# Forming two operand sums of a ConvFFN in PSUM and placing two steps of a third weight job ahead of them

## The chip, the cores and the metric

The kernel runs on one core of a Trainium2 chip. The metric is the device time of one execution in microseconds (us); the figure for a kernel is the median over its runs. Engines are named as the profile names them: PE is TensorE, DVE is VectorE, ACT is ScalarE, POOL is GpSimd, SP is SyncE. In this kernel SP issues nearly all of the DMAs.

## The reference

One layer of an encoder: two attention branches are merged, projected by `w_out` and added to the residual; then comes a ConvFFN whose input is a norm of that residual. The part around the change, with D_MODEL 1024, SEQ 1024, D_FF 2816 and everything in float32:

```python
x = x + gate1 * (merged @ w_out[i])
h2 = rmsnorm(x, g_ffn[i]) * (1 + scale2) + shift2
u = depthwise_conv_seq(h2 @ w_up[i], conv_w[i], conv_b[i])      # width 3, over positions
u_val, u_gate = jnp.split(u, 2, axis=-1)
x = x + gate2 * ((jax.nn.gelu(u_gate, approximate=True) * u_val) @ w_down[i])
return rmsnorm(x, g_final)
```

## The kernel before

**Number format.** A float32 operand is split into `hi` (the value rounded to the matmul's format) and `lo` (the rest). Every product is three matmuls: hi by hi, hi by lo, lo by hi (lines 77 to 79 in the projections, 916 to 918 in the later part). `split` does this for weights: ACT writes `hi` (line 55), DVE or POOL writes `lo` (line 56). `operand` (lines 862 and 863) does it for activations, and `shifted` (lines 1036 and 1037) does it while adding a shift per partition.

**Fewer products.** `h2 @ w_up` is done with seven products of half-size blocks in place of eight (a Strassen-Winograd scheme). `STEPS` names the seven: ("11","B11"), ("S2","T2"), ("S1","T1"), ("S3","T3"), ("12","B21"), ("S4","B22"), ("22","T4"). The first name is the weights' side, the second the activations' side. T2, T1, T3 and T4 are sums and differences of the two halves of the normed residual; S1 to S4 are sums of weight blocks, made by `a_operands` (POOL makes S1, S2 and a21, lines 880 to 882). `w_up` has 22 jobs (t = 0 to 21), each with two weight tiles of 512 KB (`up_load`, line 1064). The activations' operands are made once and serve all jobs. A job has seven steps of 12 matmuls (`products`), and the chain of sums behind them is done by ACT and DVE (lines 922 to 938). Each job ends in the convolution (`conv_in` on ACT, line 1105; six `conv_taps` for each of the two halves on DVE, line 1111), a gelu (line 1137), a multiply (line 1138) and a store (line 1139).

**Order.** Positions are done in two halves. The projection by `w_out` runs for the first half, whose norm gives `m1` and B11, B21; then for the second half, which gives `m2`. At the second norm the sums of squares go to a column on PE (`add_sums`, line 89), `rstd_of` makes the reciprocal root (lines 94 to 96), and `bcast` spreads it over the partitions by four transposes (line 102) into the PSUM tile `pbc`. Then `m2` is multiplied by it (line 1179), and T2, T1, T3, B22 and T4 are formed in a loop written out by hand. From there the order of PE is by hand too (`late_mm`), up to step 1 of the first two jobs. `gens[t]` yields after two of the four k-tiles of each step (-1) and after each step; `advance` runs one to the end of its step. The first two jobs go in the order (0, 4, 1, 2, 3, 5, 6), because steps 0 and 4 need only B11 and B21. Everything outside these hand-ordered blocks is put in order by a planner from estimated durations; each engine and queue then executes its list strictly in order.

**Buffers.** PSUM has six banks under `pj` and one each under `pcol` and `pbc`. `big` has nine buffers of 4 KB a partition, `wc` (`wide()`) five of 2 KB, and `wraw` (raw weights) two. Before the change the sums T2 lie in one `big` and two `wc`, and T1 overwrites `m1`:

```python
dve.tensor_tensor(m2[k], m2[k], bc, OP.mult)                    # line 1179
dve.tensor_tensor(t2[k - 1], m2[k - 1], m1[k - 1], OP.add)      # line 1181
dve.tensor_tensor(m1[k - 5], m2[k - 1], t2[k - 5], OP.subtract) # line 1183
```

Of the kernel before, what the change touches and what calls it, by code (L numbers as in the profile page):

```python
# [28 lines left out]
def hybrid_encoder(tc, xT, c, w_ada, small, w_in, w_v, p1_bias, p23_bias, na_bias, ln2_mult, ident, w_br, w_out,  # L29
# [69 lines left out]
    def bcast(r, psum_pool, tag, n=4):  # L99
        pb = psum_pool.tile([128, 512], FT, name="pbc", tag=tag)  # L100
        for t in range(n):
            pe.transpose(pb[:, t * 128:(t + 1) * 128], r[:, t:t + 1].to_broadcast([128, 128]), idt)
        return pb
# [757 lines left out]
    def operand(t, hi, lo, lo_eng):  # L861
        act.activation(hi, t, AF.Copy)
        lo_eng.tensor_tensor(lo, t, f(hi), OP.subtract)
# [5 lines left out]
    def a_operands(raw, n, work, st, lo_eng=pool, last=False):  # L869
# [12 lines left out]
        pool.tensor_tensor(a21, a11, a21, OP.subtract)  # L882
        hi, lo = (wpool.tile([128, KT, 128], FR, name=t).rearrange("p (a b) m -> p a b m", a=2)[:, :, :n]
                  for t in ("whi", "wlo"))
        pair(raw[0], ("11", "12"), hi, lo, lo_eng)
# [140 lines left out]

    oppools = [tc.alloc_tile_pool(name=n, bufs=1, reuse_waits="tile") for n in ("B11", "B21")]
    ops = {n: [p.tile([128, 4, 512], FR, name=n + e) for e in ("hi", "lo")] for n, p in zip(("B11", "B21"), oppools)}
    x_scr = dram.tile([KT, 128, S], FT, name="xs")
    a_scr = dram.tile([FF, 128, S], FT, name="as")  # L1030
    shift2 = ada[:, 24:32]
# [27 lines left out]

    def up_load(t):  # L1060
        raw = []
        for i in range(2):
            r = big([128, KT, 128]) if t in (0,) or t > 1 and t % 2 else wpool.tile([128, KT, 128], FT, name="wraw")
            sp.dma_start(r, w_up[t + FF * i])
# [16 lines left out]
        shifted(m1[k], shift2[:, k:k + 1], hi[:, k % 4], lo[:, k % 4])  # L1081

    m2 = []
    sqa = wide()
    for m in range(KT - 1):
        m2.append(half_tile())
        out_tile(1, m, sqa, m2[m])
        if m == 3:
# [3 lines left out]
    sts = [{} for _ in range(FF)]  # L1092
# [10 lines left out]
    with tc.tile_pool(name="up", bufs=2, reuse_waits="tile") as work:  # L1103
# [15 lines left out]
        def up_products(t, st, seq=range(7)):  # L1119
            u, ys = [{}, {}], {i: big([128, S]) for i in range(2) if t == FF - 1}  # L1120

            def done(i, hf, src):
                u[i][hf] = src
                if len(u[i]) == 1 and t < 2:
                    return
                with tc.high_priority(offset=-300 if t == FF - 1 else 0):
                    finish(i, hf)

            def finish(i, hf):
                if i not in ys:  # L1130
                    ys[i] = big([128, S])
                for n in range(2) if t < 2 else (hf,):
                    conv_in(ys[i], t + FF * i, n, u[i][n])
                if len(u[i]) == 2:
                    conv_taps(ys[i], t + FF * i, u[i])
                if len(u[0]) + len(u[1]) == 4:
                    act.activation(ys[1], ys[1], AF.Gelu_apprx_tanh)  # L1137
# [29 lines left out]
        t2 = big([128, 2, 512])  # L1167
        t2 = [t2[:, 0], t2[:, 1], wide(), wide()]

        def t_split(n, k, src, b):  # L1170
            shifted(src, b, ops[n][0][:, k], ops[n][1][:, k])

        with tc.manual_schedule(engines={act.engine, dve.engine, pool.engine}):

            for k in range(10):
                if k == 3:
                    dve.tensor_tensor(m2[3], m2[7], m2[3], OP.subtract)
                if k < 8:
                    dve.tensor_tensor(m2[k], m2[k], bc, OP.mult)
                if 1 <= k < 5:  # L1180
                    dve.tensor_tensor(t2[k - 1], m2[k - 1], m1[k - 1], OP.add)
                elif k >= 5 and k < 9:
                    dve.tensor_tensor(m1[k - 5], m2[k - 1], t2[k - 5], OP.subtract)
                if 2 <= k < 6:
                    t_split("T2", k - 2, t2[k - 2], shift2[:, 2 + k:3 + k])
                elif k >= 6:
                    operand(m1[k - 6], ops["T1"][0][:, k - 6], ops["T1"][1][:, k - 6], dve)
            for k in range(4):
                t_split("T3", k, m2[k], dshift[:, k:k + 1])
                pool.tensor_tensor(m1[4 + k], m1[4 + k], t2[k], OP.subtract)  # L1190
            for k in range(4):
                late["B22"].append((half_tile(FR), half_tile(FR)))
                shifted(m2[4 + k], shift2[:, 4 + k:5 + k], *late["B22"][k])
            for k in range(4):
                late["T4"].append((half_tile(FR), half_tile(FR)))
                operand(m1[4 + k], *late["T4"][k], pool)
        for g in gens:
            advance(g)
        late_mm.close()
        for t in range(FF):  # L1200
            nxt = iter(())
            if t + 2 < FF:
                raw[t + 2] = up_load(t + 2)
            if 0 < t < FF - 1:
                nxt = a_operands(raw.pop(t + 1), 4, lambda t: work, sts[t + 1], last=t + 2 == FF)
                next(nxt)
            elif t == 0:
                nxt = prep[1]
            for j in gens[t] if t < 2 else up_products(t, sts[t]):
                if j in (((2, 5), (2, 3, 5))[t] if t < 2 else (1, 2, 5)):  # L1210
                    next(nxt, None)
                if t == FF - 1 and j == 0:
                    more = b_operands(0, movs[0])
                    next(more)
                if t == FF - 1 and j == 2:
                    next(more)
                if t == FF - 1 and j == 3:
                    oppool2.release()
                    work2 = tc.alloc_tile_pool(name="down2", bufs=1, side="right", reuse_waits="tile")
                    reserve(work2, [(n + e, 2048, G) for n in ("B11", "T2", "T1") for e in "hl"]  # L1220
                            + [("T3h", 2048, G), ("T3l", 2048, G)])
                    for _ in range(3):
                        next(more)
    for p in oppools[::-1]:
        p.release()

    x3 = {}
# [202 lines left out]
```

## Time and profile before

| | |
|---|---|
| median of 3 runs | 1549.67 us (1546.57 to 1551.87) |
| profiled execution | 1549.12 us, span 1547.3 us |
| mean granted PE clock | 0.983 |
| busy PE / DVE / ACT / POOL | 96% / 66% / 52% / 50% of the span |

Times inside the profile count from the start of the span. The projection's second half ends at 869.3 us, the second norm and the sums lie between 869 and 903 us, and the 22 jobs of `w_up` run on from there. A timeline row gives start, duration, engine, line and operation, output tile and inputs, shapes and count; in square brackets stands how long the engine was idle before it, and what released it. Rows that hold several instructions (x2 and more) give the stretch from the first start to the last end. Tiles carry the name of their buffer, so the normed residual `m2` shows as `x`, and T2's sums as `big` and `wc`.

### The profile page before, as it was taken

The page shows a single profiled execution, that of the slowest core. Times are in us where ns is not written, and L with a number is a line of the kernel's source. Part 1 is how long each engine was busy: PE and PEld are TensorE (multiplying, and loading weights), DVE is VectorE, ACT ScalarE, POOL GpSimd, SP SyncE. Part 2 cuts the span into 40 slices and gives each one's busy share as a digit, 9 for nine tenths or more (in the row PEclk, how much of TensorE's full clock was granted, in tenths as well). Part 3 has the DMA queues.
Part 4 walks back from the last instruction along what each step waited for, and adds up shares of the span by engine and source line. Part 5 has one row for each costly group of instructions (what it writes and reads, how often), then busy time and mean ns, then how long its engine had stood idle before and what let it go on. Part 6 is the DMA issues. An engine that isn't in the chain of part 4 may idle for free.

```text
span 1547.3 us, 21066 instructions
## 1 busy us (share of the span) xinstructions
PE 1489.8 (96%) x7512; PEld 1256.8 (81%) x7512; DVE 1016.6 (66%) x1862; ACT 804.4 (52%) x1461; POOL 778.1 (50%) x500
## 2 busy tenths in 40 slices
PE   6999999999999999999999899999999999999998
PEld 5778888888988998888778677888888887788787
DVE  6664457676766665535535898777777776887775
ACT  5542656565765766643335454444444446575542
POOL 3525434332224554311156859767776665778621
PEclk7999999999999999999999989999999999999999
DMA  9857234423434465555544213222222223623312
GB/s 342 343 203 260 69 104 131 115 80 101 133 112 139 132 161 153 155 193 174 170 139 143 86 55 110 91 87 82 82 82 82 82 75 137 206 94 124 115 55 110
DMA packets 109873, 205.20 MB, mean 133 GB/s; under 512 B 40228, under 2 KB 55460, under 8 KB 109732
## 3 DMA queue, kind: packets, MB, share of 16 engines
q1 hardware_dynamic: 109496, 203.59, 40.6%
q8 instruction: 59, 0.97, 0.3%
q14 instruction: 46, 0.38, 0.1%
q10 hardware_dynamic: 272, 0.26, 0.0%
HBM read 158.73 MB, written 42.47 MB: 130 GB/s over the span
## 4 chain that ended last, share of the span: by engine, by line
PE 76%; DVE 9%; POOL 4%; DMA 4%; issue 3%; ACT 3%; SPq 0%; DVEq 0%; ACTq 0%; POOLq 0%
PE pj L916 10%; PE pj L918 10%; PE pj L917 10%; PE pj L79 10%; PE pj L78 10%; PE pj L77 10%; PE pj L467 2%; PE O L768 2%; DVE big L1111 1%; POOL wlo L56 1%; PE T L756 1%; PE S L735 1%; PE b L247 1%; DMA g<-gs 1%; PE b L249 1%
## 5 line engine op out<-in xcount | busy, mean ns | idle before, releaser
L56 POOL TENSOR_TENSOR wlo<-wraw,whi 128x1024 fp32r<-128x1024 f32 (+1 forms) x77 | 179.2, 2328 | 246.3 <-ACT whi L55 245.0
L78 PE MATMUL pj<-h,whi 128*128 128x512 f32 x448 | 178.0, 397 | 0.0
L79 PE MATMUL pj<-h,wlo 128*128 128x512 f32 x448 | 178.0, 397 | 0.0
L77 PE MATMUL pj<-h,whi 128*128 128x512 f32 x448 | 177.9, 397 | 0.0
L1111 DVE SCALAR_TENSOR_TENSOR big<-pj,sm,big 128x512 f32<-128x512 f32 (+2 forms) x252 | 128.5, 566 | 33.1 <-ACT big L1105 33.1
L56 POOL TENSOR_TENSOR wsl<-big,wsh 128x1024 fp32r<-128x1024 f32 (+1 forms) x45 | 109.8, 2441 | 55.7 <-ACT wsh L55 54.6
L1105 ACT ACTIVATE big<-pj,sm 128x512 f32<-128x512 f32 x84 | 63.1, 776 | 123.1 <-DVE pj L934 55.1
L55 ACT ACTIVATE whi<-wraw 128x1024 fp32r<-128x1024 f32 (+1 forms) x79 | 80.7, 1022 | 83.1 <-PE pj L78 30.0
L79 PEld LDWEIGHTS pj<-h,wlo 128*128 128x128 f32 x448 | 84.3, 188 | 14.4
L78 PEld LDWEIGHTS pj<-h,whi 128*128 128x128 f32 x448 | 84.3, 188 | 14.1
L77 PEld LDWEIGHTS pj<-h,whi 128*128 128x128 f32 x448 | 84.3, 188 | 13.8
L538 POOL TENSOR_TENSOR vv<-vv 96x256 fp32r<-96x256 f32 (+2 forms) x32 | 41.1, 1295 | 99.8 <-ACT vv L537 98.1
L594 ACT ACTIVATE P<-P,st 128x256 f32<-128x256 f32 x128 | 64.3, 503 | 51.7 <-DVE st L593 51.4
L593 DVE CUSTOM_DVE_ANT_0 P<-S,bias 128x256 f32<-128x256 f32 x128 | 52.4, 421 | 43.4 <-PE S L640 24.6
L746 POOL TENSOR_SCALAR P<-P,stb 128x288 f32<-128x288 f32 (+1 forms) x32 | 39.9, 1248 | 66.3 <-DVE stb L743 57.7
L55 ACT ACTIVATE wsh<-big 128x1024 fp32r<-128x1024 f32 (+1 forms) x45 | 44.9, 1001 | 42.2 <-POOL big L881 20.5
L1138 DVE TENSOR_TENSOR big<-big 128x1024 f32<-128x1024 f32 x22 | 49.3, 2241 | 23.3 <-ACT big L1137 23.3
L474 POOL TENSOR_SCALAR qb<-qs 128x256 fp32r<-128x256 f32 x32 | 26.4, 851 | 71.4 <-PE S L640 58.6
L56 POOL TENSOR_TENSOR wsl<-wraw,wsh 128x768 fp32r<-128x768 f32 (+1 forms) x23 | 54.2, 2354 | 12.8 <-ACT wsh L55 12.6
L599 DVE TENSOR_TENSOR tl<-T,th 128x512 fp32r<-128x512 f32 x64 | 43.7, 688 | 22.8 <-ACT th L598 22.3
L889 DVE TENSOR_TENSOR wraw<-wraw,big 128x384 f32<-128x384 f32 (+1 forms) x23 | 36.4, 1582 | 33.3 <-POOL big L881 30.4
L79 PE MATMUL pj<-mhi,wlo 128*128 128x512 f32 x128 | 50.8, 397 | 1.9 <-POOL wlo L56 1.9
(377 smaller groups left out, 4810.3 us busy)
## 6 DMA issues: line engine op xcount, KB each, us to landing
t<-w_ada SPq DMA_DIRECT2D x40, 512.0 KB, 6.5
wraw<-w_in SPq DMA_DIRECT2D x32, 512.0 KB, 5.7
big<-w_up SPq DMA_DIRECT2D x22, 512.0 KB, 5.2
wraw<-w_up SPq DMA_DIRECT2D x22, 512.0 KB, 3.5
as<-big SPq DMA_DIRECT2D x22, 512.0 KB, 2.7
big<-as SPq DMA_DIRECT2D x22, 512.0 KB, 6.6
wraw<-w_down SPq DMA_DIRECT2D x24, 384.0 KB, 3.6
gs<-gs SPq DMA_DIRECT2D x32, 256.0 KB, 2.1
```

What stands on the lines that cost most here:

```text
L55: act.activation(hi, raw, AF.Copy)
L56: lo_eng.tensor_tensor(lo, raw, f(hi), OP.subtract)
L77: pe.matmul(psum, whi[:, k0 + k], mhi, start=k == 0, stop=False)
L78: pe.matmul(psum, whi[:, k0 + k], mlo, start=False, stop=False)
L79: pe.matmul(psum, wlo[:, k0 + k], mhi, start=False, stop=k == n - 1)
L593: dve.tensor_tensor_reduce(pp, d, bias, -1.0, BIG, OP.add, OP.min, mi)
L594: act.activation(pp, pp, AF.Exp, bias=mi, scale=-1.0, accum_out=li)
L916: pe.matmul(psum, whi[:, k], bhi, start=j < 4 and k == 0, stop=False, skip_group_check=True)
L917: pe.matmul(psum, whi[:, k], blo, start=False, stop=False, skip_group_check=True)
L918: pe.matmul(psum, wlo[:, k], bhi, start=False, stop=k == n - 1, skip_group_check=True)
L1105: act.activation(y[:, halves[hf]], src, AF.Identity, bias=conv[:, 3, t:t + 1], scale=conv[:, 1, t:t + 1])
L1111: dve.scalar_tensor_tensor(y[:, dst], src, wt, y[:, dst], OP.mult, OP.add)
```

## The change

At the second norm:

- ACT copies `m1` into a PSUM tile for each of the four k (`staged`: `pj` banks for even k, the `pcol` bank for odd k). DVE adds `m2` to it there, so T2's sum is in PSUM. ACT makes `hi` from it and copies the sum back over `m1`; DVE makes `lo` from it. T1's difference is written to PSUM as well, and `hi` and `lo` are made from there. The tile `t2` (one `big`, two `wc`) is gone; the subtraction `m2[3] = m2[7] - m2[3]` comes first in the block.
- Job t = 2 gets its first weight tile (`w3`, blocks 11 and 12) during the projection's second half. It is held in a `big` buffer in place of a `wraw`, and its hi and lo are put in a new pool `third` (two tiles of 6 KB a partition). The same split later, in `a_operands`, falls away.
- Job 2's step 0 is put ahead of the first T2 step, and its step 4 between the T2 steps of jobs 0 and 1. Job 2 now has the order (0, 4, 1, 2, 3, 5, 6) and, as jobs 0 and 1, starts each half's convolution only when both parts of it are there.
- The first six matmuls of job 1 come ahead of the broadcast in place of behind it.

```diff
     def up_load(t):
         raw = []
-        for i in range(2):
+        for i in range(t == 2, 2):
...
-        return raw
+        return [w3, *raw] if t == 2 else raw
...
         out_tile(1, m, sqa, m2[m])
+        if m == 0:
+            w3 = big([128, 2, 4, 128])
+            sp.dma_start(w3, w_up[2].rearrange("p (a b) m -> p a b m", a=2))
+        if m == 1:
+            hi, lo = (t[:, 0:2].rearrange("p i (a m) -> p i a m", a=4) for t in third)
+            split(w3, hi, lo, pool)
...
-                if len(u[i]) == 1 and t < 2:
+                if len(u[i]) == 1 and t < 3:
...
-        gens = [up_products(t, sts[t], (0, 4, 1, 2, 3, 5, 6)) for t in range(2)]
+        gens = [up_products(t, sts[t], (0, 4, 1, 2, 3, 5, 6)) for t in range(3)]
...
         advance(gens[0])
+        next(gens[1])
         bc = bcast(rstd_of(pcol, 4), ps, "pbc")
-        advance(gens[1])
-        advance(gens[0])
-        advance(gens[1])
+        for g in (1, 0, 1, 2):
+            advance(gens[g])
+        def staged(k):
+            return ps.tile([128, 512], FT, name="stage", tag="pcol") if k % 2 else \
+                ps.tile([128, 512], FT, name="pj", bufs=6)
...
+            def copied(k):
+                t2[k] = staged(k)
+                act.activation(t2[k], m1[k], AF.Copy)
+            copied(0)
+            copied(1)
+            dve.tensor_tensor(m2[3], m2[7], m2[3], OP.subtract)
+            for k in range(5):
+                if k < 4:
+                    dve.tensor_tensor(m2[k], m2[k], bc, OP.mult)
+                    dve.tensor_tensor(t2[k], t2[k], m2[k], OP.add)
+                    act.activation(ops["T2"][0][:, k], t2[k], AF.Identity, bias=shift2[:, 4 + k:5 + k])
+                    act.activation(m1[k], t2[k], AF.Copy)
+                if k:
+                    dve.scalar_tensor_tensor(ops["T2"][1][:, k - 1], t2[k - 1], shift2[:, 3 + k:4 + k],
+                                             f(ops["T2"][0][:, k - 1]), OP.add, OP.subtract)
+                    if k < 3:
+                        copied(k + 1)
+            for k in range(5):
+                if k < 4:
+                    dve.tensor_tensor(m2[4 + k], m2[4 + k], bc, OP.mult)
+                    t1[k] = staged(k)
+                    dve.tensor_tensor(t1[k], m2[4 + k], m1[k], OP.subtract)
+                    act.activation(ops["T1"][0][:, k], t1[k], AF.Copy)
+                if k:
+                    dve.tensor_tensor(ops["T1"][1][:, k - 1], t1[k - 1], f(ops["T1"][0][:, k - 1]), OP.subtract)
...
-        for g in gens:
-            advance(g)
+        for g in (0, 2, 1):
+            advance(gens[g])
```

More of the change, by code (lines that the diff above doesn't have):

```diff
@@ L867, in hybrid_encoder, with a_operands @@
     names = tuple(b for _, b in STEPS)
-    def a_operands(raw, n, work, st, lo_eng=pool, last=False):
+    def a_operands(raw, n, work, st, lo_eng=pool, last=False, first=True):
         a11, a12, a21, a22 = raw[0][:, 0], raw[0][:, 1], raw[1][:, 0], raw[1][:, 1]
@@ L882, in a_operands @@
         pool.tensor_tensor(a21, a11, a21, OP.subtract)
-        hi, lo = (wpool.tile([128, KT, 128], FR, name=t).rearrange("p (a b) m -> p a b m", a=2)[:, :, :n]
-                  for t in ("whi", "wlo"))
-        pair(raw[0], ("11", "12"), hi, lo, lo_eng)
+        if first:
+            hi, lo = (wpool.tile([128, KT, 128], FR, name=t).rearrange("p (a b) m -> p a b m", a=2)[:, :, :n]
+                      for t in ("whi", "wlo"))
+            pair(raw[0], ("11", "12"), hi, lo, lo_eng)
         yield
@@ L1028, in hybrid_encoder @@
     ops = {n: [p.tile([128, 4, 512], FR, name=n + e) for e in ("hi", "lo")] for n, p in zip(("B11", "B21"), oppools)}
+    third_pool = tc.alloc_tile_pool(name="third", bufs=1, reuse_waits="tile")
+    third = [third_pool.tile([128, 3, 512], FR, name="w3" + n) for n in "ab"]
     x_scr = dram.tile([KT, 128, S], FT, name="xs")
@@ L1083, in hybrid_encoder @@
     m2 = []
+    sts = [{} for _ in range(FF)]
     sqa = wide()
@@ L1087, in hybrid_encoder @@
         out_tile(1, m, sqa, m2[m])
+        if m == 0:
[4 more added lines that the diff above has]
+            split(w3, hi, lo, pool)
+            for i, name in enumerate(("11", "12")):
+                sts[2][name] = hi[:, i], lo[:, i]
         if m == 3:
@@ L1131, in finish @@
                     ys[i] = big([128, S])
-                for n in range(2) if t < 2 else (hf,):
+                for n in range(2) if t < 3 else (hf,):
                     conv_in(ys[i], t + FF * i, n, u[i][n])
@@ L1161, in hybrid_encoder @@
         advance(gens[0])
+        next(gens[1])
         bc = bcast(rstd_of(pcol, 4), ps, "pbc")
-        advance(gens[1])
-        advance(gens[0])
-        advance(gens[1])
[L1167 to L1171, printed above, removed]
-        with tc.manual_schedule(engines={act.engine, dve.engine, pool.engine}):
[L1175 to L1187, printed above, removed]
+        for g in (1, 0, 1, 2):
+            advance(gens[g])
@@ L1204, in hybrid_encoder @@
             if 0 < t < FF - 1:
-                nxt = a_operands(raw.pop(t + 1), 4, lambda t: work, sts[t + 1], last=t + 2 == FF)
+                nxt = a_operands(raw.pop(t + 1), 4, lambda t: work, sts[t + 1], last=t + 2 == FF, first=t > 1)
                 next(nxt)
@@ L1208, in hybrid_encoder @@
                 nxt = prep[1]
-            for j in gens[t] if t < 2 else up_products(t, sts[t]):
-                if j in (((2, 5), (2, 3, 5))[t] if t < 2 else (1, 2, 5)):
+            for j in gens[t] if t < 3 else up_products(t, sts[t]):
+                if j in ((2, 5) if t == 0 else (2, 3, 5) if t < 3 else (1, 2, 5)):
                     next(nxt, None)
@@ L1223, in hybrid_encoder @@
                         next(more)
-    for p in oppools[::-1]:
+    for p in (third_pool, *oppools[::-1]):
         p.release()
```

6 lines of the change are left out of this document (3 added, 3 removed).

## The prediction, made before the change was run

> **What bounds the kernel now.** I start with the page's engine line and then ask where PE waits.
>
> ```profile
> PE 1489.8 (96%) x7512; PEld 1256.8 (81%) x7512; DVE 1016.6 (66%) x1862; ACT 804.4 (52%) x1461; POOL 778.1 (50%) x500
> ```
>
> PE is busy 96% of the span, so only a stage in which PE stands can give anything. The list of waits, for 862 to 910 us and then for 910 to 960, names such a stage:
>
> ```profile
> PE pj L917 <- DVE T2lo L1037: 5.5, 3, 2.7
> PE pbc L102 <- DVE rs L96: 1.8, 1, 1.8
> PE pj L917 <- DVE T1lo L863: 0.3, 1, 0.3
> ...
> PE pj L916 <- ACT wc L922: 2.7, 1, 2.7
> ```
>
> Busy time by stretches (columns: PE, PEld, DVE, ACT, POOL, granted PE clock, DMA share, GB/s) adds two things: the clock falls behind those waits, and DVE is full.
>
> ```profile
> 888.60:899.20 10.60, 7.83 (x18) 5.17 (x19) 10.60 (x12) 3.17 (x6) 6.80 (x4) 0.52 0.15 49
> ...
> 903.00:938.70 35.70, 35.70 (x158) 29.20 (x157) 33.44 (x41) 17.82 (x25) 26.61 (x15) 1.00 0.23 81
> 938.70:941.70 3.00, 0.33 (x2) 0.11 (x1) 1.82 (x3) 1.70 (x3) 0.26 (x1) 1.00 0.23 87
> 943.00:970.00 27.00, 27.00 (x121) 22.37 (x120) 20.15 (x27) 12.99 (x17) 27.00 (x15) 1.00 0.36 117
> ```
>
> In 888.6 to 899.2 the granted clock is 0.52 and DVE is busy without a break: PE waits for DVE to form T2. From 903 PE is full but for one wait at 938.7; from 943 it is full again, with DVE busy 75% of the time. What PE gains before 943 and does not lose again there should therefore reach the end. PE's timeline prices the stage:
>
> ```profile
> 873.62 0.39 PE L918 MATMUL pj<-B11hi,wlo 128*128 128x512 f32 x1
> 875.86 0.62 PE L102 MATMUL pbc<-idt,rs 128*128 128x128 f32 x4 [1.85 <-DVE rs L96]
> 876.24 0.47 PE L916 MATMUL pj<-B11hi,whi 128*128 128x512 f32 x1
> ...
> 884.58 0.39 PE L916 MATMUL pj<-T2hi,wsh 128*128 128x512 f32 x1
> ...
> 899.90 0.40 PE L916 MATMUL pj<-T1hi,wsh 128*128 128x512 f32 x1
> ```
>
> From 876.24 to 884.58 PE runs 36 matmuls, 0.23 us each. The next 24 (two T2 steps) take 884.58 to 899.90, 15.3 us, where 24 x 0.23 = 5.5 would do: 9.8 us are lost, 5.5 of them waits and 4.3 the slow clock. With 1.85 at the broadcast and 0.33 at T1, 12.0 us are there to be had; the wait at 938.7 is another 2.7.
>
> **The change, part by part.** The sums first: DVE's groups by shape, 876 to 912 us (the last two columns before the idle time are busy us and mean ns), then rows of its timeline.
>
> ```profile
> L1179 DVE TENSOR_TENSOR x<-x,pbc 128x512 f32<-128x512 f32 x8 | 5.4, 679 | 0.8 <-PE pbc L102 0.8
> L1181 DVE TENSOR_TENSOR big<-x,big 128x512 f32<-128x512 f32 x2 | 4.9, 2447 | 0.0
> L1183 DVE TENSOR_TENSOR big<-x,wc 128x512 f32<-128x512 f32 x2 | 3.1, 1530 | 0.0
> L863 DVE TENSOR_TENSOR T1lo<-big,T1hi 128x512 fp32r<-128x512 f32 x4 | 2.6, 678 | 0.0
> L1037 DVE SCALAR_TENSOR_TENSOR T2lo<-big,ada,T2hi 128x512 fp32r<-128x512 f32 x2 | 2.5, 1264 | 0.0
> L1037 DVE SCALAR_TENSOR_TENSOR T2lo<-wc,ada,T2hi 128x512 fp32r<-128x512 f32 x2 | 2.5, 1246 | 0.0
> L1181 DVE TENSOR_TENSOR wc<-x,big 128x512 f32<-128x512 f32 x2 | 1.9, 932 | 0.0
> L1183 DVE TENSOR_TENSOR big<-x,big 128x512 f32<-128x512 f32 x2 | 1.8, 922 | 0.0
> L1177 DVE TENSOR_TENSOR x<-x,x 128x512 f32<-128x512 f32 x1 | 1.8, 1771 | 0.0
> ```
> ```profile
> 876.52 1.29 DVE L1179 TENSOR_TENSOR x<-x,pbc 128x512 f32<-128x512 f32 x2 [0.81 <-PE pbc L102]
> ...
> 902.47 2.73 DVE L1037 SCALAR_TENSOR_TENSOR T3lo<-x,cols,T3hi 128x512 fp32r<-128x512 f32 x4
> ...
> 914.39 0.70 DVE L934 TENSOR_TENSOR pj<-pj,wc 128x512 f32<-128x512 f32 x1
> ```
>
> The multiplies, one input of which is the PSUM tile `pbc`, all take 0.68 us. The adds of line 1181 have the same shape with both inputs in SBUF, and take up to 2.4. POOL explains it:
>
> ```profile
> 874.60 7.99 POOL L56 TENSOR_TENSOR wsl<-big,wsh 128x1024 fp32r<-128x1024 f32 x3
> 882.55 3.44 POOL L1190 TENSOR_TENSOR big<-big 128x512 f32<-128x512 f32 x2
> ```
>
> POOL works all through the slow adds. So an add with its sum in PSUM should take what line 934 takes (PSUM and SBUF in, PSUM out), 0.70 us. The Trainium skill, "SBUF — State Buffer", section "Who interferes with whom", states this as a rule: a DVE instruction with two SBUF inputs contends with a GpSimd instruction that reads SBUF, one with at most one does not. The rows agree for the adds; by the same rule T1's subtractions, whose inputs both stay in SBUF, gain nothing from a result in PSUM.
>
> DVE's sum. Before, to 902.47: adds 6.8, T2's lo 5.0, multiplies 5.4, T1's subtractions 4.9, T1's lo 2.6, the subtraction of line 1177 1.8: 26.5 us. After: adds 4 x 0.70 = 2.8; T2's lo, now from PSUM, 4 x 0.74 = 2.9 (T3's uncontended form, 2.73 for four, is the nearest row); multiplies 5.4; T1's subtractions 4.9, kept; T1's lo 2.6; line 1177's 1.8, now ahead of the multiplies and so in front of T2, begun at 875.8 where DVE waited for the broadcast. ACT's part is new in the chain:
>
> ```profile
> 875.41 0.58 ACT L922 ACTIVATE wc<-pj 128x512 f32<-128x512 f32 x1
> ...
> 880.36 0.73 ACT L1036 ACTIVATE T2hi<-big,ada 128x512 fp32r<-128x512 f32 x1 [4.37 <-DVE big L1181]
> ```
>
> Per k ACT has hi (0.73), the copy back (0.58) and one copy ahead (0.58), about 1.9 us against DVE's 2.1 (multiply, add, lo). Since the copy for k + 1 stands behind hi and the copy back of k, I let DVE wait 0.7 us at k = 2 and at k = 3, 1.4 in all. After: 21.8 us. Bound for this: nothing at ACT and 0.7 a subtraction gives 18.3, every subtraction as slow as the slowest add gives 26.7. The rows before overlap by 1.9 us (26.5 and two line 924 rows of 0.68 in 25.95), so the chain ends at 875.8 + 21.8 + 1.4 - 1.9 = 897.1 where it ended at 902.47: **DVE is 5.4 us earlier.**
>
> T2's four lo come out at 880.7, 883.4, 886.0 and 886.8 (first multiply at 877.5; per k multiply and add 1.3, hi 0.7, lo 0.7).
>
> PE's part. Six matmuls come ahead of the broadcast: PE is free at 873.85 + 6 x 0.23 = 875.2, DVE is done with the reciprocal at 875.7 (it is idle the 0.81 us before 876.52), so the broadcast stays at 875.86 and 0.5 of the 1.85 us wait is left. Behind it stand 6 + 12 + 12 + 12 = 42 matmuls, 9.7 us, to 885.9. T2's k-tiles are wanted at 885.9, 886.6, 887.3 and 888.0: all are there. Then come job 2's step 4 and the second T2 step, to 894.2. T1 is wanted from 894.2, its last k-tile at 896.3, and DVE gives it at 897.1: 0.8 us of waiting, no stretch long enough for the clock to fall as it did. So of 12.0 us 1.3 stay: **PE is 10.7 us ahead at T1.** The matmuls pulled ahead are not new work; they leave job 2.
>
> Loads and weights. SP issues one 512 KB load earlier, POOL and ACT do one split earlier.
>
> ```profile
> 859.58 2.40 POOL L56 TENSOR_TENSOR wlo<-wraw,whi 128x1024 fp32r<-128x1024 f32 x1 [1.31 <-ACT whi L55]
> ...
> 896.02 2.38 POOL L56 TENSOR_TENSOR wlo<-wraw,whi 128x1024 fp32r<-128x1024 f32 x1 [2.99 <-ACT whi L55]
> ...
> 891.36 18.31 SPq L1064 DMA_DIRECT2D wraw<-w_up  x2
> 909.77 0.86 SPq L1064 DMA_DIRECT2D big<-w_up  x2
> ```
>
> The split (2.38 us on POOL) moves from 896 into the projection, where POOL idles 1.3 us ahead of a split of `w_out`, which PE waits for in turn: between 0 and 2.4 us, I take 0, because the planner can put it in any gap up to 883, where it is first used. Behind the moved load SP's queue gets shorter: job 2's second tile need no longer wait for the second `wraw` (the end of the 18.3 us, 909.4) but takes the first (891.4). Job 2's S1 and S2 come 18 us earlier than before while PE wants them some 11 earlier. I cost this at nothing; its cover is that slack.
>
> What is late next. At 938.7 PE waits for the evacuation that stands behind a gelu on ACT, and the gelu for six taps on DVE:
>
> ```profile
> 940.00 1.06 ACT L1137 ACTIVATE big<-big 128x1024 f32<-128x1024 f32 x1 [9.47 <-DVE big L1111]
> ...
> 930.65 9.26 DVE L1111 SCALAR_TENSOR_TENSOR big<-wc,sm,big 128x256 f32<-128x256 f32 x6
> ...
> 921.59 2.20 DVE L1111 SCALAR_TENSOR_TENSOR big<-wc,sm,big 128x512 f32<-128x512 f32 x4 [0.37 <-ACT big L1105]
> ```
>
> Six taps with both inputs in SBUF took 9.26 us, four others 2.20, so six need not take over 3.4. DVE is 33.4 of 35.7 us busy here, and it moves up by 5.4 us where PE moves up by 10.7. If the taps are as slow again, PE meets DVE here and is 5.4 us ahead in the end; if they are quick, PE keeps 10.7 and saves the 2.7 too: 13.4. Nothing says which, since POOL's order is planned anew; I take half of the 5.9 us between the taps' two prices: 5.4 + 2.9, rounded to **8.4 us**.
>
> The sum: 1549.12 - 8.4 = 1540.7 for the profiled execution; the median stands 0.55 above that execution, so 1541.2, given as 1541.0.
>
> **Rivals.**
>
> *The stall moves from T2 to T1* (chance 0.16). T1's subtractions keep both inputs in SBUF, and POOL's m1 differences now fall beside them. If each takes the 2.45 us of line 1181, a k-tile costs 0.6 + 2.45 + 0.63 = 3.7 us, and T1's last is there near 886.8 + 4 x 3.7 = 901.6 in place of 896.3: 5.3 us of waiting, and another 4.3 if the clock falls again. Of 12.0 us 2.4 are left: 1546.7 to 1547.3, no change. For it speaks that line 1183 took 1.53 on average on `wc`; against it, 0.92 on `big`. The Trainium skill, "TensorE: Matmul & The Clock Gate", Part 1, has the clock fall after an idle window of about 3.4 us; here it fell with no single wait over 2.7, and did not at 938.7 after one of 2.7, so the trace does not separate one long wait from several short ones. By that page the 4.3 would not be added, and the time would be 1543.
>
> *The ninth buffer* (chance 0.09, the other side). `w3` holds a `big` from the projection until job 2's S4 is split, and job 3's two tiles need two.
>
> ```profile
> big<-w_up SPq DMA_DIRECT2D x22, 512.0 KB, 5.2
> ...
> 934.36 1.74 POOL L56 TENSOR_TENSOR big<-wraw,big 128x512 fp32r<-128x512 f32 x1
> ...
> 942.57 2.41 POOL L56 TENSOR_TENSOR wsl<-big,wsh 128x1024 fp32r<-128x1024 f32 x1 [3.61 <-ACT wsh L55]
> ```
>
> That split ends at 936.1 now. If job 3's second load waits for it, it lands 5.2 us later (the page's median for these loads), three POOL sums of 1.72 (two of line 1190 took 3.44), a hi of 1.06 and a lo of 2.4 follow, and S2 is ready at 950.0 where it was at 945.0. All that was gained is lost, 5.0 more, and 4.3 for a clock that falls: 1549.7 + 9.3 = 1559.0. It decides from a load issued later than about 931; now it goes at 909.8. Against it: `t2`'s `big` is gone, and with S2 18 us earlier the split can be as well.
>
> *All of it stays* (inside the forecast's range): 13.4 us, 1536.3.
>
> **How the numbers follow.** The three runs of before spread by 5.3 us, 0.34%, so a change under about 0.3% (4.65 us) can't be told. The forecast (5.4 to 13.4 us, 1536.3 to 1544.3) has 0.71; the stall at T1 0.16; the ninth buffer 0.09; 0.04 is for a gain that POOL's split in the projection (2.4) brings under the limit, counted as no change. Faster 0.71, same 0.20, slower 0.09. The range reaches from the whole gain and a little more, 1535.5, over the T1 rival to 1548.0; what lies above is the ninth buffer and the worst of the unchanged.
>
> **What would show it.** The adds at 0.7 us beside a busy POOL; T1's subtractions still up to 2.4; one wait of about 0.5 us at the broadcast, none at T2, about 0.8 at T1; a granted clock of 1.00 throughout; the chain of sums over near 897; a wait of PE for DVE or for an evacuation near 925 to 935. The prediction is wrong if T2 still waits (ACT's copies are slower than 0.6 us or stand behind something else), if PE waits in the projection for POOL, or if a load of job 3 goes out after 930.

## The result: slower by 0.6%, and the profile after

The changed kernel takes 1558.34 us (median of six runs, 1557.1 to 1559.88); the kernel before takes 1548.55 us beside it (six runs, 1545.23 to 1551.87). The ratio is 1.0062, interval 1.0048 to 1.0077: 9.8 us slower, where 8.4 us of gain were forecast, and above the range's upper end of 1548.0.

The engine line of the page after. PE is busy for 3.9 us more than before, although it runs the same 7512 instructions:

```profile
PE 1493.7 (96%) x7512; PEld 1259.6 (81%) x7512; DVE 1011.7 (65%) x1862; ACT 807.4 (52%) x1469; POOL 775.0 (50%) x500
```

To compare two traces I count from one event that both have, the first matmul of the second norm's column sums (line 89): 869.30 us before, 869.46 us after. I call it t0. Busy time by stretches from t0, with the number of matmuls in brackets behind PE and the granted clock three columns from the end; first the kernel before:

```profile
869.30:889.30 20.00, 15.43 (x76) 12.10 (x74) 18.76 (x19) 9.56 (x14) 18.05 (x9) 0.99 0.03 14
889.30:909.30 20.00, 16.90 (x58) 12.42 (x57) 20.00 (x24) 11.72 (x18) 8.49 (x6) 0.75 0.08 27
909.30:929.30 20.00, 20.00 (x90) 16.41 (x89) 17.74 (x28) 10.65 (x14) 14.82 (x10) 1.00 0.22 79
929.30:949.30 20.00, 17.33 (x77) 14.02 (x76) 16.64 (x15) 8.74 (x12) 16.39 (x9) 1.00 0.47 159
949.30:979.30 30.00, 30.00 (x134) 24.86 (x133) 23.96 (x36) 12.22 (x15) 25.92 (x15) 1.00 0.17 56
```

and the kernel after:

```profile
869.46:889.46 20.00, 16.07 (x75) 13.37 (x74) 14.44 (x16) 11.32 (x19) 16.71 (x9) 0.91 0.03 13
889.46:909.46 20.00, 16.06 (x68) 12.16 (x67) 17.65 (x28) 13.26 (x23) 4.84 (x4) 1.00 0.09 27
909.46:929.46 20.00, 17.66 (x76) 13.92 (x75) 15.79 (x19) 9.23 (x11) 17.73 (x11) 1.00 0.21 79
929.46:949.46 20.00, 14.51 (x51) 11.18 (x52) 18.80 (x21) 7.71 (x11) 13.00 (x8) 0.83 0.33 111
949.46:979.46 30.00, 30.00 (x134) 24.82 (x133) 19.80 (x35) 12.97 (x17) 22.68 (x14) 1.00 0.19 67
```

The stage that the change was made for did get better: in its second stretch PE runs 68 matmuls at a clock of 1.00 where it ran 58 at 0.75. But not in the first stretch, and the two stretches behind it are worse: 76 and 51 where there were 90 and 77. From t0 + 80 us on both are full and alike (134 and 134). Counted in one stretch from t0, so that none at an edge counts twice, the kernel after is 10 matmuls ahead at t0 + 40 (142 against 132) and 27 behind at t0 + 80 (268 against 295). A matmul takes 0.2275 us at full clock: 2.3 us of lead have become 6.1 us of lag. From t0 to the end of the span it is 688.0 us against 678.0, so another 3.9 us come later; they are not placed (see the end of the experiments).

The list of PE's waits, first for 862 to 910 us and then for 910 to 960 us (us in total, times, longest). Before, it was 5.5 at T2's lo, 1.8 at the broadcast, 0.3 at T1, and one of 2.7 later:

```profile
PE pbc L102 <- DVE rs L96: 3.9, 1, 3.9
PE pj L917 <- ACT T2hi L1196: 2.7, 1, 2.7
PE pj L917 <- DVE wc L925: 1.3, 2, 0.9
...
PE pj L917 <- DVE wc L939: 3.8, 1, 3.8
PE pj L917 <- DVE big L1122: 2.1, 2, 1.1
PE pj L917 <- DVE wc L927: 1.9, 1, 1.9
```

The waits for T2's lo are gone, but the broadcast's wait has doubled though six matmuls stand in front of it, PE still waits 2.7 us for T2, and there are three new ones later. DVE's timeline shows the first two:

```profile
873.77 2.71 DVE L890 TENSOR_TENSOR wraw<-wraw,big 128x512 f32<-128x512 f32 x1
876.39 0.15 DVE L94 TENSOR_SCALAR rs<-pcol 128x4 f32<-128x4 f32 x1
876.47 2.76 DVE L1191 TENSOR_TENSOR x<-x,x 128x512 f32<-128x512 f32 x1
879.15 0.16 DVE L96 RECIPROCAL rs<-rs 128x4 f32<-128x4 f32 x1
880.58 0.69 DVE L1194 TENSOR_TENSOR x<-x,pbc 128x512 f32<-128x512 f32 x1 [1.27 <-PE pbc L102]
883.98 0.70 DVE L1195 TENSOR_TENSOR pj<-pj,x 128x512 f32<-128x512 f32 x1 [2.71 <-ACT pj L1187]
...
888.67 0.70 DVE L1195 TENSOR_TENSOR pj<-pj,x 128x512 f32<-128x512 f32 x1 [1.36 <-ACT pj L1187]
...
892.16 0.70 DVE L1195 TENSOR_TENSOR stage<-stage,x 128x512 f32<-128x512 f32 x1 [1.55 <-ACT stage L1187]
...
894.10 0.75 DVE L1199 SCALAR_TENSOR_TENSOR T2lo<-stage,ada,T2hi 128x512 fp32r<-128x512 f32 x1 [0.59 <-ACT big L1197]
...
902.02 0.69 DVE L1210 TENSOR_TENSOR T1lo<-stage,T1hi 128x512 fp32r<-128x512 f32 x1
```

Read it from the top. The subtraction of line 1191, which nothing needs before the fourth k-tile of T2, stands on DVE between the column's scaling (line 94) and the reciprocal (line 96). Both its inputs are in SBUF and POOL is busy, so it takes 2.76 us, and the reciprocal, the broadcast and PE wait for it. Then the multiply is done, and the first add waits 2.71 us for ACT's copy, the third 1.36, the fourth 1.55. The adds themselves take 0.70 us, as forecast. The last T1 lo ends at 902.7 us: nothing is gained there against 902.47 before. ACT's timeline shows why the copies are late:

```profile
882.85 0.60 ACT L923 ACTIVATE wc<-pj 128x512 f32<-128x512 f32 x1 [5.07 <-PE pj L919]
883.35 0.60 ACT L1187 ACTIVATE pj<-big 128x512 f32<-128x512 f32 x1
...
891.04 0.60 ACT L923 ACTIVATE wc<-pj 128x512 f32<-128x512 f32 x1 [0.46 <-PE pj L919]
891.53 0.59 ACT L1187 ACTIVATE stage<-big 128x512 f32<-128x512 f32 x1
```

ACT idles for 5.07 us at an evacuation (line 923): job 1's step 0, whose last matmuls stand on PE behind the late broadcast. The copies of line 1187, whose input `m1` has long been there, stand behind it in ACT's list. The same happens once more at 891. On PE the two long waits look like this, and the granted clock behind the first (a row that takes 0.63 us in place of 0.39) falls:

```profile
879.46 1.09 PE L102 MATMUL pbc<-idt,rs 128*128 128x128 f32 x4 [3.92 <-DVE rs L96]
...
880.77 0.63 PE L918 MATMUL pj<-B11lo,whi 128*128 128x512 f32 x1
...
893.65 0.47 PE L917 MATMUL pj<-T2hi,wsh 128*128 128x512 f32 x1 [2.66 <-ACT T2hi L1196]
...
931.90 0.76 PE L917 MATMUL pj<-T3hi,wsh 128*128 128x512 f32 x1 [3.80 <-DVE wc L939]
```

The one at 931.9 waits for an evacuation by DVE, which has these instructions in front of it:

```profile
922.55 5.03 DVE L1122 SCALAR_TENSOR_TENSOR big<-wc,sm,big 128x512 f32<-128x512 f32 x2
927.50 2.85 DVE L890 TENSOR_TENSOR big<-big 128x512 f32<-128x512 f32 x1
...
931.06 0.69 DVE L939 TENSOR_TENSOR wc<-pj,wc 128x512 f32<-128x512 f32 x1
```

Two taps and one subtraction, all with both inputs in SBUF beside a busy POOL, take 7.8 us; a subtraction of this size takes 0.70 us elsewhere (line 1207, 900.65 us, where POOL is idle).

### The profile page after: what moved, and what is told of

Same layout as the page of the kernel before. It is cut to its first block, busy times and chain, and to the rows that moved or that the text cites. A ratio compares the mean times of both kernels' runs of the same rounds, so it can differ in the third digit from the quotient of the medians.

```text
span 1557.5 us, 21073 instructions
## 1 busy us (share of the span) xinstructions
PE 1493.7 (96%) x7512; PEld 1259.6 (81%) x7512; DVE 1011.7 (65%) x1862; ACT 807.4 (52%) x1469; POOL 775.0 (50%) x500
## 5 line engine op out<-in xcount | busy, mean ns | idle before, releaser
L1122 DVE SCALAR_TENSOR_TENSOR big<-pj,sm,big 128x512 f32<-128x512 f32 (+2 forms) x252 | 128.7, 566 | 33.2 <-ACT big L1116 33.2
L55 ACT ACTIVATE whi<-wraw 128x1024 fp32r<-128x1024 f32 (+1 forms) x78 | 79.7, 1022 | 87.2 <-PE pj L78 33.4
L55 ACT ACTIVATE wsh<-big 128x1024 fp32r<-128x1024 f32 (+1 forms) x45 | 44.8, 1000 | 37.0 <-PE pj L918 18.2
```

Of the source, the lines that this page charges most:

```text
L55: act.activation(hi, raw, AF.Copy)
L1122: dve.scalar_tensor_tensor(y[:, dst], src, wt, y[:, dst], OP.mult, OP.add)
```

## The experiments

In what follows "ahead" and "behind" are matmuls since t0 against the 132 and 295 of the kernel before at t0 + 40 and t0 + 80. t0 itself lies between 864.0 and 871.2 us in these profiles, so times are compared from t0. Each count comes from one profile of a kernel; the one kernel that was profiled twice (c_evac and c_evac5) gives 170 and 170 matmuls at t0 + 40, 309 and 308 at t0 + 80. The experiments were run in three series, beside which the kernel before took 1550.75, 1549.37 and 1549.35 us, where it took 1548.55 beside the changed kernel. So ratios are compared, and not times; the expectations name times, which are to be read in the same way.

**a_sub: the subtraction leaves its place in front of the reciprocal.**

```diff
-            dve.tensor_tensor(m2[3], m2[7], m2[3], OP.subtract)
             for k in range(5):
                 if k < 4:
...
                     act.activation(m1[k], t2[k], AF.Copy)
+                if k == 2:
+                    dve.tensor_tensor(m2[3], m2[7], m2[3], OP.subtract)
                 if k:
```

> The changed kernel with one DVE instruction moved: the subtraction m2[3] = m2[7] - m2[3] stands behind the third add in place of first in the block; nothing else in any engine's order differs. Theory Q (two instructions that stand in front on their in-order engines make the sums late, and what is lost in jobs 1 to 3 follows from DVE being late): the reciprocal follows the column's scaling at once (876.6 in place of 879.15), the broadcast's wait falls from 3.9 to about 1.4 us, the granted clock stays at 1.00 there, and the time falls by about 3 us, to 1555. Rival D (jobs 1 to 3 lose by the order of POOL, SP and the contended taps, whatever T2 does): the T2 steps start 2 to 3 us earlier, but the waits between 915 and 950 grow by as much and the time stays within 1 us of 1558.

Measured: 1556.27 us, ratio to before 1.0034 (1.0022 to 1.0045), against 1.0062 for the whole change. PE's wait at the broadcast is 1.6 us where it was 3.9; the one for T2 is 2.7 as before. 14 behind at t0 + 80 in place of 27. The subtraction's place cost about 0.28% (4.3 us), a little more than the 3 us that theory Q gives it.

**a_copy: the copies go ahead of the evacuation on ACT.** The two first copies are issued right behind the broadcast, before the steps that PE runs ahead of T2.

```diff
         bc = bcast(rstd_of(pcol, 4), ps, "pbc")
+        t2, t1 = {}, {}
+        def copied(k):
+            t2[k] = staged(k)
+            act.activation(t2[k], m1[k], AF.Copy)
+        copied(0)
+        copied(1)
         for g in (1, 0, 1, 2):
             advance(gens[g])
...
```

> The changed kernel with ACT's order changed alone: the copies of m1[0] and m1[1] into PSUM are issued ahead of the evacuation of job 1's step 0, and the fourth copy comes out ahead of that of job 2's step 0; DVE's order is the same. Theory Q: the first add no longer waits 2.7 us for a copy that stands behind an evacuation that waits for PE, nor the fourth 1.5; T2's last lo is ready about 4 us earlier (890 to 891 in place of 894.8), the 2.7 us wait before T2 is gone, and the time is about 1554. Rival D: T2 and T1 are earlier by as much, but the time is 1557 to 1558.

Measured: 1557.32 us, ratio 1.0041 (1.0026 to 1.0055). The wait for T2 is gone from the list, the one at the broadcast is 3.9 as it was. 17 behind at t0 + 80. The gain of 0.21% (3.3 us) lies between the two theories (about 4 us and about 1).

**a_both: the two together.**

> The changed kernel with both: subtraction behind the third add, first two copies ahead of the evacuation. Theory Q: the two add up, T2 is complete near 888, PE has no wait at T2, and the time is 1550 to 1552. Rival D: T2 and T1 without waits, but jobs 1 to 3 lose what was gained: 1556 to 1558.

Measured: 1552.86 us, ratio 1.0017 (1.0002 to 1.0032). The two parts bring 0.28% and 0.21% alone, and 0.45% together: within their intervals they add up, as two separate causes do, and as theory Q has it. For 862 to 910 us PE's list of waits has 1.6 us at the broadcast and 2.3 at `wc L925`, none at T2. Two rows of DVE's timeline (the first multiply and T1's last lo; t0 is 866.55 us):

```profile
874.88 0.69 DVE L1193 TENSOR_TENSOR x<-x,pbc 128x512 f32<-128x512 f32 x1 [0.81 <-PE pbc L102]
...
892.51 0.69 DVE L1211 TENSOR_TENSOR T1lo<-stage,T1hi 128x512 fp32r<-128x512 f32 x1
```

The sums end at t0 + 26.6 us, where they ended at t0 + 33.2 before and after the change alike. PE is 34 matmuls (7.7 us) ahead at t0 + 40. That is the gain that the prediction worked for; yet at t0 + 80 the count is 2 behind. So a second question arises: where do these 8 us go?

**b_sums and b_both: the sums alone.** The kernel before with the new sums and without the third job and the later broadcast; in b_both with both mends of a_both.

> The kernel before with the new sums alone (T2 and T1 formed in PSUM, with ACT's copies and the subtraction first); no third job's steps, the broadcast where it was. Theory Q: the adds take 0.7 us each, the subtraction in front still delays the reciprocal by 2 to 3 us, and PE, which has nothing to run there, waits for that and for T2: 1547 to 1551. Rival D (the loss comes with the third job's steps and loads): the same range, 1545 to 1549. Rival S (the sums in PSUM themselves bring the loss downstream, through ACT's queue): 1554 or more.

> The sums in PSUM with both mends (subtraction behind the third add, first two copies ahead), but no third job's steps and the broadcast where it was: a_both without its other two parts. Theory B (job 2 begun early holds PSUM banks that jobs 0 and 1 need, and that is where jobs 1 to 3 lose): without job 2's steps PE waits some 3 to 4 us more at T2 than a_both, but loses only the 2.7 us of before further on, and the time is at or below that of before, ratio 0.996 to 1.000. Rival T (DVE is the bound of the stage; job 2's steps are a gain as they are): the wait at T2 is paid in full and the ratio is above a_both's 1.0017.

Measured: b_sums 1554.78 us, ratio 1.0027 (1.0014 to 1.004); b_both 1549.17 us, ratio 1.0006 (0.9992 to 1.002). The first lies between the ranges of theories Q and S, the second between B and T. The waits of b_sums at the broadcast and for 910 to 960 us:

```profile
PE pbc L102 <- DVE rs L96: 4.2, 1, 4.2
...
PE pj L916 <- ACT wc L922: 6.0, 1, 6.0
```

The sums alone make the kernel slower, with the broadcast as late as in the whole change. The 6.0 us end with an evacuation that stands in ACT's list behind a gelu, which had waited 5.53 us for DVE's taps. Mended (b_both) they put PE 15 ahead at t0 + 40, though it waits 3.4 us for T1's lo there, and 1 behind at t0 + 80: one wait of 4.5 us for a weight tile (`ACT wsh L55`) takes the lead back. That split, too, stands on ACT behind a gelu that had waited for the taps, 4.75 us. In the end they are worth nothing that can be told from no change.

**a_nosums: the other part alone.** The changed kernel with the sums of before, so the third job's steps, its early load and split, and the later broadcast.

> The changed kernel with the old sums (T2 in SBUF, the old loop and the old place of the subtraction): the third job's steps, its load and split, and the later broadcast alone. Theory Q (the new sums' orders on DVE and ACT are what costs): without them the broadcast waits 0.5 us, T2's last operand comes at 894 as before, PE fills 24 matmuls of the waits, and the ratio is 0.997 to 1.000. Rival J (the third job's steps and loads cost as much as they give): 1.002 to 1.004, so that with the sums' 1.0027 it makes up the 1.0062.

Measured: 1552.85 us, ratio 1.0016 (1.0000 to 1.0032). It waits 3.7 us for T2's lo (before 5.5) and 1.6 at the broadcast, is 16 ahead at t0 + 40 and 11 behind at t0 + 80. The ratio lies between the ranges of both theories. The parts give 0.27% and 0.16%; together 0.43% of the 0.62%. This part too gains where it was meant to and loses that and more between t0 + 40 and t0 + 80.

**c_bank: do jobs 0 to 2 hold too many PSUM banks?** Job 2's convolution now waits for both of its parts, so it may keep a bank that job 3 needs. a_both, with job 2's sums put in SBUF as those of jobs 0 and 1:

```diff
-                            seq, t > 1)
+                            seq, t > 2)
```

> a_both with job 2 writing its sums to SBUF (wc) as jobs 0 and 1 do, in place of keeping them in PSUM: its bank b comes free at once. Theory B: the 3.6 us wait for DVE's line 939 and the slow clock behind it are gone, the time falls by 3 to 5 us against a_both (ratio to before 0.998 to 1.000). Rival T (DVE bound): the wait moves to the next bank, the ratio stays at 1.001 to 1.002.

Measured: 1549.16 us, ratio 1.0003 (0.9989 to 1.0017). The time is a little better than a_both's, with intervals that overlap, but the wait that this theory was made for, `DVE wc L939`, is 3.6 us in both kernels, and both are 2 and 1 behind at t0 + 80. The theory falls.

**c_evac: the second T2 step's evacuation goes ahead of B22's operands on DVE.** In a_both PE's largest wait in the stage is for `wc L925`. This evacuation stands behind B22's four operands, 3.76 us together, because these are in the hand-ordered block and it comes behind the block. a_both, with

```diff
+            for g in (0, 2, 1):
+                advance(gens[g])
             for k in range(4):
                 late["B22"].append((half_tile(FR), half_tile(FR)))
...
-        for g in (0, 2, 1):
-            advance(gens[g])
```

> a_both with the evacuations of the two T2 steps (line 925) ahead of B22's four operands on DVE in place of the second one behind them. Theory E (a third instruction that stands behind others on DVE): the 1.8 us wait at the bank of T1 is gone, DVE no longer idles 2.3 us for PE, and the time falls by 2 us against a_both, ratio 1.000. Rival T: the wait is paid later, ratio 1.001 to 1.002.

> c_evac (all three orders mended) once more against the kernel before, in five rounds, since its interval took in 1.000: by its profile, 2.5 us shorter behind the column sums than before, the ratio should be 0.998 to 0.999; if the 2.5 us are chance of one execution, 1.000.

Measured: 1547.66 us, ratio 0.9989 (0.997 to 1.0008), and for the same kernel once more (c_evac5) 1546.62 us, ratio 0.9979 (0.9964 to 0.9994). The first interval takes in no change, the second does not: this version beats the kernel before by 0.1 to 0.2%, and the changed kernel by 0.7 to 0.8% by way of the ratios. What the third move brings by itself is less sure, as the intervals of a_both (1.0002 to 1.0032) and c_evac overlap. The waits of c_evac for 862 to 910 and for 910 to 960 us:

```profile
PE pbc L102 <- DVE rs L96: 1.6, 1, 1.6
PE pj L917 <- DVE wc L925: 1.1, 1, 1.1
...
PE pj L917 <- ACT wc L923: 2.9, 1, 2.9
PE pj L917 <- DVE big L1122: 2.2, 1, 2.2
PE pj L917 <- DVE wc L930: 1.1, 1, 1.1
```

38 ahead (8.6 us) at t0 + 40, 14 ahead (3.2 us) at t0 + 80. The largest of the later waits is the one that the kernel before has at 938.7 us: an evacuation behind a gelu on ACT behind the taps on DVE.

**c_evacbank: c_evac and c_bank together.**

> a_both with both of these. Theories B and E together: 5 to 7 us below a_both, ratio 0.997 to 0.998. Rival T: 1.001 to 1.002.

Measured: 1549.29 us, ratio 1.0002 (0.9987 to 1.0018): no better than either, so beside c_bank's edit (1.0003) the move of c_evac brings nothing. It is 19 ahead at t0 + 80 and 7 ahead at t0 + 110, so here the loss comes later.

**d_notaps and b_notaps: are the taps what takes the lead?** c_evac, and the kernel before, without the convolution taps of jobs 0 and 1, so that the outputs of these jobs lack the neighbouring positions:

```diff
-                if len(u[i]) == 2:
+                if len(u[i]) == 2 and t > 1:
```

> c_evac with the convolution's taps of jobs 0 and 1 left out (24 DVE instructions; those two jobs' outputs lack the neighbours). Theory V (in jobs 1 to 3 DVE is the bound: what the sums gain, PE loses again waiting for DVE): the waits of PE between 915 and 945 (6.2 us, and the slow clock behind the last) go, PE keeps the 6 to 8 us that it is ahead 50 us behind the column sums, and the time falls by 5 to 8 us against c_evac, ratio 0.994 to 0.996. Rival W (the weights' loads and splits of jobs 2 and 3 on SP, ACT and POOL are the bound): the waits stay, under another name, and the ratio is within 0.001 of c_evac's 0.999.

> The kernel before with the same taps left out, as the control. Theory V: DVE is late there too, but PE waits for it only 2.7 us, so at most 2.7 us are gained: ratio 0.998 to 0.999. Rival W: no change, 1.000. If it gains as much as d_notaps does against c_evac, neither theory explains where the gain of the sums goes.

Measured: d_notaps 1545.04 us, ratio 0.9971 (0.9956 to 0.9985); b_notaps 1546.07 us, ratio 0.9985 (0.997 to 1.0). At t0 + 80 d_notaps has 322 matmuls and b_notaps 305: 27 and 10 ahead. Without taps c_evac gains 13, the kernel before 10. And from t0 + 40 to t0 + 80 the lead of c_evac over before goes from 38 to 14, that of d_notaps over b_notaps from 41 (173 against 132) to 17. It is the same 24 matmuls, 5.5 us, with the taps and without them. So the taps are a cost of both kernels, but not the place where this lead goes, and as the expectation of b_notaps says, neither theory explains it. The largest wait of d_notaps for 910 to 960 us (two others are 0.6 and 0.5), one stretch of 10 us, three rows of ACT and one of POOL:

```profile
PE pj L917 <- ACT wsh L55: 2.5, 1, 2.5
...
920.20:930.20 10.00, 7.55 (x25) 5.78 (x26) 6.05 (x3) 6.41 (x9) 10.00 (x5) 0.83 0.14 55
...
918.51 1.04 ACT L55 ACTIVATE whi<-big 128x1024 fp32r<-128x1024 f32 x1
919.46 1.04 ACT L55 ACTIVATE whi<-wraw 128x1024 fp32r<-128x1024 f32 x1
...
921.07 1.04 ACT L55 ACTIVATE wsh<-big 128x1024 fp32r<-128x1024 f32 x1
...
919.63 2.50 POOL L56 TENSOR_TENSOR wlo<-big,whi 128x1024 fp32r<-128x1024 f32 x1 [5.37 <-ACT whi L55]
```

DVE is free here (busy for 6.05 of 10 us) and POOL is full from 919.63 on. But PE's wait, from 919.65 to 922.16, is not for POOL: it ends with ACT's `hi` of job 2's S2 and S1 (the row at 921.07). POOL had the two sums done at 913.0 and then stood idle for 5.37 us. ACT works without a break from 914.75 us, and in its list this split stands behind a gelu and behind the splits of two later jobs' first tiles, job 3's (918.51), which PE first reads at 924.89, and job 4's (919.46), which PE first reads at 952.82. With the slow clock behind the wait (eight matmuls in 3.45 us, where 1.82 would do) it costs 4.1 of the 5.5 us. So in this kernel most of the lead seems to go at the place of an instruction in ACT's list once more; the wait for POOL is 0.5 us.

What stays open: that is read from one trace, and no experiment moves the split. Nor does one take back what brings job 4's split so far forward, the order of the weights' loads (see the loads, below). And between t0 + 80 and the end single profiles are later than their count at t0 + 80 says, by 0.2 us (b_notaps) to 4.0 us (a_copy), 3.9 for the changed kernel and 7.0 for c_evacbank; what makes that part was not found.

## Why the prediction was wrong, step by step

- *Adds at 0.70 us beside a busy POOL*: right. In the changed kernel POOL is busy beside the third add only, as the others come late; in a_both it is busy beside all four, and each takes 0.70. *T2's lo at 0.74*: right. *T1's subtractions still slow, 4.9 us for four*: wrong to the good side, 2.8. POOL's own differences (line 1213) were done at 895.4 us and POOL then idled until 907.5, so nothing contended. The rule about two SBUF inputs (the Trainium skill, "SBUF — State Buffer", "Who interferes with whom") holds on both sides: 0.70 us with POOL idle, 2.76 with POOL busy. A result in PSUM doesn't change that: in b_sums one of T1's subtractions took 2.78 us beside a split on POOL. In the changed kernel the rival of a stall at T1 didn't come about for the same reason; in b_sums and b_both PE did wait for T1's lo, 2.9 and 3.4 us.
- *Line 1177's subtraction, "begun at 875.8 where DVE waited for the broadcast"*: **this step failed first.** I put it into an idle stretch that lies behind the reciprocal. In the trace it lies in front of it, so it makes the idle stretch: the broadcast came at 879.46, not 875.86. a_sub prices it at 0.28%. The mistake was to place a moved instruction by when its engine is idle, when the engine's list decides.
- *"I let DVE wait 0.7 us at k = 2 and at k = 3"*: **this step failed next.** I counted ACT's busy time per k (hi, copy back, copy ahead) and not what else stands in ACT's list. The waits are 2.71, 1.36, 1.55 and 0.59: 6.2 us in place of 1.4. The sum behind the 897.1 also counts its 1.4 us twice: the 21.8 us have them already, and by its own terms the chain would end at 875.8 + 21.8 - 1.9 = 895.7. The two errors explain most of the end of the sums, 902.7 in place of 897.1: 3.1 us later at the first multiply (880.58 against 877.5), 3.4 more of waiting than the 2.8 in the sum, 2.1 less for the subtractions; the other 1.2 are mostly rows that overlap by 0.8 us in place of 1.9. a_both, without the two, ends at t0 + 26.6, which is 895.9 on the clock of before.
- *Broadcast at 875.86 with 0.5 us of wait left*: even mended, 1.6 is left, and it comes at t0 + 7.7 in place of t0 + 6.6 (a_both). A subtraction of job 1's weights (line 890) ahead of the scaling takes 2.71 us where it took 1.60; both its inputs are in SBUF. POOL is busy beside it before and after, but with other splits: those of 128 x 1024 start 2 us earlier than before (872.55 against 874.60). In a_both, c_evac and d_notaps it takes 2.71 too, in b_sums and b_both, without the third job's part, 1.60. Why one split slows it more than the other was not tried. I had taken DVE's work up to there as fixed.
- *PE 10.7 us ahead at T1*: at t0 + 30, where PE before comes to T1, the count is 16 matmuls or 3.6 us ahead in the kernel as it is, 41 or 9.3 us in a_both. At t0 + 40 it is 10 in the kernel as it is, 34 in a_both and 38 in c_evac. What c_evac mends, a T2 evacuation that stands behind B22's operands, is in no step of the prediction.
- *What is late next, "5.4 us ahead in the end ... 13.4"*: the place was right, PE meets DVE near 925 to 935 and again at the evacuation behind the gelu; the size was not. Even with the first errors mended the gain in the end is 0.1 to 0.2%, 2 to 3 us, under the lower end of 5.4. The prediction took the taps as the one thing there; in d_notaps, without them, PE loses as much, by the trace most of it to a split on ACT that stands behind others.
- *Loads and weights at nothing*: wrong. SP's queue did get shorter at one place, and no load of job 3 goes out after 930, so the rival of the ninth buffer falls too; that its 1559.0 us lie next to the measured time is chance. SP's loads, POOL's rows up to job 2's sums, and two splits on ACT:

```profile
888.54 27.88 SPq L1067 DMA_DIRECT2D wraw<-w_up  x2
916.52 0.85 SPq L1067 DMA_DIRECT2D big<-w_up  x2
...
907.49 6.22 POOL L863 TENSOR_TENSOR x<-big,x 128x512 fp32r<-128x512 f32 x4 [12.04 <-ACT x L862]
...
916.02 1.29 POOL L880 TENSOR_TENSOR big<-wraw 128x512 f32<-128x512 f32 x1
...
921.91 1.04 ACT L55 ACTIVATE whi<-wraw 128x1024 fp32r<-128x1024 f32 x1
922.86 1.04 ACT L55 ACTIVATE wsh<-big 128x1024 fp32r<-128x1024 f32 x1
```

  Job 2's second tile is issued at 888.54 us, as forecast, where it was the second `wraw` before (909.4). But the sums that need it begin at 916.02 where they began at 915.38. POOL stands idle for 12.04 us in front of T4's four lo, which wait for ACT's hi, and job 2's sums stand behind these in POOL's list. The 18 us that I named as this edit's cover never reached PE. And job 3's two loads go out 6.7 us later (916.52 in place of 909.77), as they stand in SP's list behind the second `wraw`, the end of the 27.88 us stretch. That second `wraw` is job 4's first tile: job 2 needs only one here, and job 3 has none. It waits for the `wraw` of job 1 that POOL's split frees at 916.06, behind T4's four lo. Then job 4's split (921.91 on ACT, 2.84 us from 924.46 on POOL) goes ahead of job 2's own (922.86 on ACT, 927.26 on POOL), though PE first reads job 4's at 964.35; before, ACT began it at 942.39. It also keeps POOL busy beside the slow taps and the subtraction of 922.55 to 930.35, in front of PE's longest later wait. What these places cost by themselves was not tried, so the order of the weights' loads and splits stays a rival for the loss between t0 + 40 and t0 + 80.
- *POOL's split in the projection, taken at 0 of 2.4 us*: nothing in the trace speaks against it. From 740 to 862 us PE waits 3.6 us for POOL's splits, 4.5 before; t0 (869.46 against 869.30 us) says little, as it varies by 7 us between profiles.
- *The clock at 1.00 throughout*: no. It is 0.91 behind the broadcast and 0.83 in 929 to 949 us, behind the waits of 3.92 and 3.80 us.

## What to carry to other kernels

When a change puts an instruction into a list that an engine executes in order, its price is not its duration: look at what stands in front of it and what stands behind it, and whether the one in front waits for an engine that the change has just made later. Here two instructions whose inputs were ready, or that nobody needed yet, cost 0.45% by their place alone; with a third moved as well, a loss of 0.6% became a gain of 0.1 to 0.2%. And a lead of 8 us on the busiest engine is worth only what the stage behind it can take: look there for what waits in each list, and for work of later jobs that an earlier load has let go in front.

## What the runs showed of the hardware

- The clock does not go by the length of a single wait. After waits of 2.67 us (before, 941.59) and 2.66 us (after, 893.65) the next matmuls come 0.23 us apart, at full clock; after one of 2.51 us (d_notaps, 922.16, nothing else idle in the 10 us before) they come 0.43 us apart for some 3 us, as they do after 2.89 us (c_evac, 937.15) and, for 2 and nearly 5 us, after 3.92 and 3.80 us (after, 879.46 and 931.90). The Trainium skill, "TensorE: Matmul & The Clock Gate", Part 1, has the clock fall after an idle window of about 3.4 us; the 2.51 us are below that. By these runs a wait from about 2.5 us up may or may not lower the clock.
- An instruction of 128 x 512 with both inputs in SBUF takes 0.70 us on DVE with POOL idle (line 1207, after, 900.65) and up to 2.85 beside POOL's splits (line 890, after, 927.50); with one input in PSUM it took 0.70 us beside a busy POOL (all four adds of a_both). A kernel in which POOL's order changes has different prices for these all over.
- The stage's start t0 lies between 864.0 and 871.2 us in profiles of the changed kernel and its variants, whose program text is the same up to there. A difference of a few us between two single profiles is therefore read from an event that both have, not from the start of the span.
